# A hybrid decoder layer: the y blocks of the second output half split ahead of the turn, the halo rows turned a tile later

## The chip, the core and the metric

The kernel runs on one core of a Trainium2 chip. The engines that matter here are TensorE (PE in the profile; its weight loads are PEld), VectorE (DVE), ScalarE (ACT) and GpSimd (POOL). All DMAs are issued from the queue of SyncE (SP). The metric is the device time of one execution in microseconds (us); lower is better.

## The reference, cut to what matters

The layer takes 1024 tokens of width 1024, with 16 meta tokens in front (1040 rows in all, float32). It consists of two sub-layers. The first projects the normalised rows and runs two head groups, a state-space mixer (SSD) and a stick-breaking attention (SB); their outputs, each of width 1024, are joined and multiplied by `w_out`, and the normalised product is added to the input. The second is a feed-forward layer with a causal convolution over three rows. The change lies in the end of the first and the way into the second:

```python
y_sb = rms_norm(stick_breaking_attention(q, k, v).reshape(Bsz, L, SB_WIDTH), sb_norm_g[l])
mix = jnp.concatenate([y_ssd, y_sb], axis=-1) @ w_out[l]
h = h + rms_norm(mix, mix_post_g[l])
xn = rms_norm(h, ffn_pre_g[l])
gu = xn @ w_up[l]
g = causal_dwconv(gu[..., :D_FF], ffn_conv_w[l], ffn_conv_b[l])
f = (jax.nn.gelu(g, approximate=True) * gu[..., D_FF:]) @ w_down[l]
```

The convolution looks two rows back, so the first token needs the last two meta rows. These two rows are the "halo" rows below.

## The kernel before, in words

Products of 32-bit accuracy are made of three matmuls: each operand is split into a high part, rounded by a copy on ScalarE, and a low part, the rest, by a subtraction on VectorE or GpSimd; high by high, low by high and high by low are added up in PSUM.

The product with `w_out` is cut into two halves by head group. The first half (SSD) runs among the attention and leaves its result in DRAM (`mixd`). The second half (SB) is the loop around the change, lines 1421 to 1493, over eight tiles t of 128 rows:

- `load_y` (line 929) loads the attention's block of tile t (`yk`, 512 KB) from DRAM. `split_y` makes its high part `yh` on ScalarE (line 938) and its low part `yl` (line 939) on VectorE or GpSimd. The blocks share two SBUF buffers (tag `wraw`) with x tiles 1 and 2 and, later, with weights; `yh` and `yl` have two buffers each.
- `out_steps` (line 951) issues 48 matmuls for a tile, 24 for each half of the columns, in four steps. Its PSUM result `mo` is scaled and added to the mix block `mb` by VectorE (`ev2`, line 1436). PSUM has two banks for `mo`.
- `after` is the norm of a tile in five steps: a square with its sum on ScalarE (line 1120) and a root on GpSimd (lines 191 and 192, `ms_mo` and `rs_mo`); two products on VectorE that give the new h (lines 1123 and 1124) and its store (1126); a second square on ScalarE (1129); a second root on GpSimd (`ms_ff`, `rs_ff`); and the product that gives the normalised rows `oxn` on VectorE (1133).
- `turn_x2`, the "turn", transposes `oxn` on TensorE (line 1139) and takes the result out of PSUM: for tiles 0 to 4 by two pairs of ScalarE copies (1145, 1146), each followed by a subtraction on VectorE (1147). Tile 0 stands for the two halo rows. Both engines read one PSUM tile, and their reads of it follow each other. Tile t is turned in the middle of the matmuls of tile t + 2.

From t = 2 on, TensorE, VectorE, ScalarE and GpSimd run in the order in which the program is written (`manual_schedule`). The order of SP's queue is made by the framework's planner, which issues a load once it reckons that a buffer is free; the queue itself is in order. In iteration t the program writes: the first 24 matmuls of tile t and `ev2`; the second root of norm t - 1; the turn of tile t - 2; the last product of norm t - 1; the split of y block t + 1; steps of the halo rows' own norm (iterations 2 to 4; their sum on VectorE is line 1199); the other 24 matmuls and `ev2`; then the first three steps of norm t. At the end of iteration 4 the halo rows are turned. At iterations 7 and 8 the first weights of the feed-forward are split (lines 1222 and 1223); behind the loop its first products (`g0a`, `u0a`, line 1294) run around the turns of tiles 7 and 8, and the feed-forward's main loop (line 1280) follows.

Of the kernel before, what the change touches and what calls it, by code (L numbers as in the profile page):

```python
# [27 lines left out]
NT = T // P  # L28
# [25 lines left out]
def tile_layer(ctx: ExitStack, tc: tile.TileContext, x, meta, rows, parts,  # L54
               w_z, w_xbc, w_dt, w_q, w_k, w_v, w_out, w_up, w_down, out):
    nc = tc.nc
# [113 lines left out]
    def run(steps, n=None):  # L170
        for _ in steps if n is None else zip(range(n), steps):
            pass
# [705 lines left out]
    def wp_f32(tag, name):  # L878
        return wp.tile([P, 8, P], F32R, tag=tag, name=name, bufs=WB).bitcast(F32).rearrange("p a b -> p (a b)")
# [46 lines left out]
    yraw = [lambda name: wp.tile([P, 8, P], F32, tag="wraw", name=name)]  # L926

    def load_y(half, t, yk):
        nc.sync.dma_start(out=yk, in_=yd1[t - 1] if half else yd[t])
        return yk  # L930

    def split_y(pool, half, t, tags, yk=None, eng=nc.gpsimd):
        nm = f"{half}_{t}"
        if yk is None:
            yk = load_y(half, t, yraw[0](f"yk{nm}"))
        yh = pool.tile([P, 8, P], F32R, tag=tags[0], name=f"yh{nm}", bufs=tags[2])
        yl = pool.tile([P, 8, P], F32R, tag=tags[1], name=f"yl{nm}", bufs=tags[2])
        nc.scalar.activation(yh, yk, AF.Copy)
        eng.tensor_tensor(yl, yk, yh.bitcast(F32), op=ALU.subtract)
        return yh, yl  # L940

    def out_steps(half, t, w, y, evac):
        yh, yl = y
        for hf in range(2):
            acc = psum_mm(f"mo{half}_{t}_{hf}")
            cs = slice(512 * hf, 512 * hf + 512)
            for k, (wh, wl) in enumerate(w):
                if k == 4:
                    yield
                for j, (u, v) in enumerate(((yh, wh), (yl, wh), (yh, wl))):  # L950
                    mm(acc, u[:, k, :], v[:, cs], start=(k == 0 and j == 0), stop=(k == 7 and j == 2))  # L951
            evac(acc, cs)
            yield
# [35 lines left out]
    for p in range(8):  # L989
        for i in range(NT):  # L990
# [30 lines left out]
            if (p, i) == (6, 3):  # L1021
                yk = [load_y(0, 1, rp.tile([P, L + 3], F32, tag="rq", name="yk0_1", bufs=3)[:, :D]
                             .rearrange("p (a b) -> p a b", b=P)),
                      load_y(0, 2, rp.tile([P, L], F32R, tag="rk", name="yk0_2", bufs=3).bitcast(F32)[:, :D]
                             .rearrange("p (a b) -> p a b", b=P))]
# [34 lines left out]
    def psum_fa(name):  # L1060
        return stage[0][1].tile([P, 2, 512], F32, tag="fa", name=name, bufs=3)

    def x2_tiles(t):
        f = psum_fa(f"x2tp{t}")
        return [f[:, hf, :].rearrange("p (b c) -> p b c", c=P) for hf in range(2)]
# [3 lines left out]
    op = opool.enter_context(tc.tile_pool(name="outp", bufs=2, side="right"))  # L1069
# [9 lines left out]
    ys = [split_y(op, 1, 1, ("yh", "yl", 2))]  # L1079
# [114 lines left out]
    def halo_sum(n):  # L1194
        r = (r_ssd, r_ssd, r_sb, r_sb)[n][:2, 0:1]
        if n == 0:
            nc.vector.tensor_scalar(halo_mt, halo_mt, r, None, op0=ALU.mult)
        else:
            nc.vector.scalar_tensor_tensor(halo_mt, halo_mo, r, halo_mt, op0=ALU.mult, op1=ALU.add)
        if n < 3:  # L1200
            nc.sync.dma_start(out=halo_mo, in_=halod[n + 1])
# [10 lines left out]
    def load_raw(j, gu, pool, tag, bufs):  # L1212
        r = pool.tile([P, KB, P], F32, tag=tag, name=f"wr{gu}{j}", bufs=bufs)
        nc.sync.dma_start(out=r, in_=w_up[j, gu])
        raws[gu, j] = r

    def pair_w(nm):
        return [wp.tile([P, KB, P], F32R, tag=f"w{e}", name=f"w{e}{nm}", bufs=WB) for e in ("hi", "lo")]
# [205 lines left out]
    for t in range(1, NT + 1):  # L1424
        if t == 2:
            order.enter_context(tc.manual_schedule(engines=ORDERED))
        if 1 < t < NT - 1:
            yk = load_y(1, t + 1, yraw[0](f"yk1_{t + 1}"))
        if mts:
            mt = mts.pop(0)  # L1430
        else:
            mt = f1.tile([P, 1032], F32, tag="gr", name=f"mb{t}", bufs=2)[:, :D]
            nc.sync.dma_start(out=mt, in_=mixd[t - 1])

        def ev2(acc, cs, mt=mt, t=t):
            nc.vector.scalar_tensor_tensor(mt[:, cs], acc, r_sb[:, t:t + 1], mt[:, cs], op0=ALU.mult, op1=ALU.add)

        if t == 5:
            b22s.append(qp.tile([P, 4, 2 * P], F32, name="b22s", tag="b22s"))
        if t < NT:  # L1440
            xt = wp_f32("wlo", f"xr{t}") if t > 2 else wp.tile([P, D], F32, tag="wraw", name=f"xr{t}")
            nc.sync.dma_start(out=xt, in_=x[(t - 1) * P:t * P, :])
        if t == 7:
            xt8 = qp.tile([P, D], F32, name="xr8", tag="xr8")
            nc.sync.dma_start(out=xt8, in_=x[T - P:, :])
            for jj in range(2):
                load_raw(jj, 0, wp, "wraw", 2)
        steps = out_steps(1, t, wres2, ys.pop(0), ev2)
        run(steps, 2)
        run(norm, 1)  # L1450
        if len(pend) > 1:
            turn = pend.pop(0)()
            run(turn, 2)
            run(norm)
            if t == NT:
                run(steps)
            run(turn)
        run(norm)
        if 1 < t < NT - 1:
            ys.append(split_y(op, 1, t + 1, ("yh", "yl", 2), yk, nc.vector if t < 5 else nc.gpsimd))  # L1460
        if t == 2:
            halo_sum(2)
        elif t == 3:
            halo_sum(3)
            halo_norm = after(0, halo_mt, 2, halo_xt, halo_mo, halo_mo)
            run(halo_norm, 1)
        elif t == 4:
            run(halo_norm)
        if t == 7:
            g0.split_1()  # L1470
            load_raw(0, 1, wp, "wraw", 2)
        elif t == NT:
            g0_pair = pair_w("2g0")
            u0.split_1()
            g0.split_2(g0_pair)
            load_raw(1, 1, wp, "wraw", 2)
        run(steps)
        if t == 6:
            edge_x2()
        if t == NT:  # L1480
            break
        if t == 6:
            ys.append(split_y(op, 1, NT, ("yh", "yl", 2)))
        xn = f1.tile([P, 1032], F32, tag="fa", name=f"oxn{t}")[:, :D]
        junk = psum_fa(f"jk{t}").rearrange("p a b -> p (a b)")
        norm = after(t, mt, P, xt, xn, junk)
        run(norm, 1)
        if t == 7:
            xt = xt8
        run(norm, 2)  # L1490
        pend.append(lambda t=t, xn=xn: turn_x2(t, P, xn, x2_tiles(t)))
        if t == 3:
            run(halo_norm, 2)
        elif t == 4:
            run(turn_x2(0, 2, halo_mo, x2_tiles(0)))
    opool.close()
    tA, tB = ExitStack(), ExitStack()
# [372 lines left out]
```

## Time and profile before

| | us |
|---|---|
| median of 3 runs | 1745.74 |
| the runs | 1743.22, 1745.74, 1745.97 |
| the profiled execution | 1741.94 |
| its span | 1740.0 |
| TensorE busy in it | 1707.8 |
| TensorE's longest wait in the second output half | 5.94 |

A row of the order of time gives start and length in us, the engine, the line of the kernel, what is written from what, and in brackets the idle time ahead of it with what ended it. Tile numbers are left out of names. A row of waits gives who waited for whom, the total in us, how often, and the longest. A row of a stretch gives the stretch, its length, the busy time of TensorE, its weight loads, VectorE, ScalarE and GpSimd with their instruction counts, the clock granted to TensorE (1.00 is full), the busy share of the DMA engines and their GB/s. "SPq" is SP issuing a DMA.

### The profile page before, as it was taken

How to read it: one execution, taken by the hardware profiler on the slowest of the kernel's cores; microseconds unless marked ns; L12 is line 12 of the kernel's file. 1: busy time of each engine (PE TensorE's matmuls, PEld its weight loads, DVE VectorE, ACT ScalarE, POOL GpSimd, SP SyncE). 2: the span in 40 equal slices, each digit the busy share in tenths (PEclk: the TensorE clock that was granted, in tenths of full speed). 3: DMA queues.
4: the chain of work that ended last, by engine and by line, in shares of the span. 5: the costliest groups of instructions: out<-in, count | busy, mean ns of one | idle time of the engine just before them, and what ended most of it. 6: DMA issues, size and time to landing. Idle time of an engine off the chain costs nothing.

```text
span 1740.0 us, 28052 instructions
## 1 busy us (share of the span) xinstructions
PE 1707.8 (98%) x11230; PEld 1496.6 (86%) x11230; DVE 1121.2 (64%) x1230; ACT 822.9 (47%) x1374; POOL 857.9 (49%) x645
## 2 busy tenths in 40 slices
PE   7999999999999999999999979999999999999998
PEld 6999889888999998998687768999988888887886
DVE  5752964775676677668532457676666666658777
ACT  5423653545566566558553234533333333343544
POOL 4323663686565566555552124487776777400001
PEclk9999999999999999999999999999999999999999
DMA  4233343231011011122215443232332222395335
GB/s 163 63 110 98 98 135 109 65 95 38 26 37 45 30 37 32 31 62 73 82 57 199 165 145 122 67 116 97 105 108 91 92 91 91 108 322 199 104 110 181
DMA packets 90694, 173.88 MB, mean 100 GB/s; under 512 B 10714, under 2 KB 35834, under 8 KB 90564
## 3 DMA queue, kind: packets, MB, share of 16 engines
q1 hardware_dynamic: 90564, 172.10, 31.2%
q8 instruction: 88, 1.44, 0.4%
q14 instruction: 42, 0.34, 0.1%
HBM read 122.33 MB, written 49.73 MB: 99 GB/s over the span
## 4 chain that ended last, share of the span: by engine, by line
PE 89%; issue 3%; DVE 3%; ACT 2%; POOL 2%; DMA 1%; POOLq 0%; DVEq 0%; SPq 0%; ACTq 0%
PE fX L1280 10%; PE dnA L1690 7%; PE fY L1280 6%; PE fA L1280 6%; PE mo L951 6%; PE pj_k L165 5%; PE pj_v L165 5%; PE pj_z L165 5%; PE dnB L1690 5%; PE pj_q L165 5%; PE pj_X L165 5%; PE av L802 4%; PE z L765 3%; PE tw L787 3%; PE pj_B L165 1%
## 5 line engine op out<-in xcount | busy, mean ns | idle before, releaser
L775 POOL TENSOR_TENSOR bt<-bt,kp 128x256 f32<-128x256 f32 (+7 forms) x128 | 213.0, 1683 | 185.5 <-DVE kp L773 135.2
L773 DVE TENSOR_TENSOR_SCAN kp<-kp,hold 128x272 f32<-128x272 f32 (+7 forms) x128 | 183.4, 1473 | 25.3 <-ACT kp L766 15.0
L1223 POOL TENSOR_TENSOR wlo<-wr,whi 128x1024 fp32r<-128x1024 f32 x43 | 107.9, 2518 | 38.4 <-ACT whi L1222 38.4
L1727 POOL TENSOR_TENSOR fms<-fms 128x1 f32<-128x1 f32 x8 | 3.2, 394 | 223.4 <-ACT dh L1612 197.0
L766 ACT ACTIVATE kp<-z 128x288 f32<-128x288 f32 (+6 forms) x112 | 82.6, 737 | 50.9 <-PE z L765 27.5
L1222 ACT ACTIVATE whi<-wr 128x1024 fp32r<-128x1024 f32 x43 | 45.6, 1060 | 111.6 <-PE fX L1280 68.3
L165 PE MATMUL pj_v<-xs,wh_v 128*128 128x400 f32 (+2 forms) x384 | 94.9, 334 | 0.0
L1352 DVE SCALAR_TENSOR_TENSOR ga<-gr,pp,ga 128x1024 f32<-128x1024 f32 x44 | 72.3, 1643 | 34.9 <-ACT ga L1345 34.1
L165 PE MATMUL pj_k<-xs,wh_k 128*128 128x400 f32 (+2 forms) x384 | 94.5, 333 | 0.0
L165 PE MATMUL pj_q<-xs,wh_q 128*128 128x386 f32 (+2 forms) x384 | 93.9, 331 | 0.0
L789 ACT ACTIVATE th<-tw 128x1024 f32<-128x1024 f32 (+2 forms) x96 | 75.6, 816 | 38.5 <-PE tw L787 38.4
L1612 ACT ACTIVATE dh<-ar 128x512 fp32r<-128x512 f32 x77 | 48.5, 630 | 92.7 <-PE dnB L1690 44.7
L165 PE MATMUL pj_X<-xs,wh_X 128*128 128x400 f32 (+2 forms) x384 | 92.0, 327 | 0.2 <-ACT craw_X L211 0.2
L165 PE MATMUL pj_z<-xs,wh_z 128*128 128x386 f32 (+2 forms) x384 | 91.5, 326 | 0.0
L951 PE MATMUL mo<-woa,yh 128*128 128x512 f32 x256 | 84.4, 398 | 2.1 <-ACT ma L963 1.2
L1613 DVE TENSOR_TENSOR dl<-ar,dh 128x512 fp32r<-128x512 f32 x77 | 53.2, 692 | 50.4 <-ACT dh L1612 50.3
L741 DVE CAST qh<-q 128x128 fp32r<-128x128 f32 x64 | 45.7, 715 | 59.7 <-PE z L765 59.4
L767 ACT ACTIVATE bt<-z 128x288 f32<-128x288 f32 (+6 forms) x112 | 82.9, 740 | 0.0
L802 PE MATMUL av<-th,v 128*64 128x128 f32 x1152 | 77.2, 278 | 0.0
L787 PE MATMUL tw<-ident,bt 128*128 128x128 f32 x576 | 75.7, 274 | 0.9 <-ACT bt L767 0.5
L802 PEld LDWEIGHTS av<-th,v 128*64 128x64 f32 x1152 | 61.5, 136 | 13.8 <-issue 11.1
L787 PEld LDWEIGHTS tw<-ident,bt 128*128 128x128 f32 x576 | 65.5, 141 | 7.1 <-issue 3.3
(558 smaller groups left out, 5648.8 us busy)
## 6 DMA issues: line engine op xcount, KB each, us to landing
wr<-in_w_up SPq DMA_DIRECT2D x44, 512.0 KB
fds<-ga SPq DMA_DIRECT2D x44, 256.0 KB
b<-in_w_down SPq DMA_DIRECT2D x44, 256.0 KB
ar<-fds SPq DMA_DIRECT2D x44, 256.0 KB
fda<-ga SPq DMA_DIRECT2D x33, 256.0 KB
ar<-fda SPq DMA_DIRECT2D x33, 256.0 KB
yk<-yd SPq DMA_DIRECT2D x16, 512.0 KB
wor<-in_w_out SPq DMA_DIRECT2D x12, 512.0 KB
```

Source lines behind the costliest of these rows:

```text
L165: mm(acc[:ncol, :n - s], a[:, k, :ncol], xs[c0][:, b, k, s:n], start=(k == 0 and j == 0), stop=(k == KB - 1 and j == 2))
L766: nc.scalar.activation(kp[:, :, a:a + w], z[:, :, :w], AF.Sigmoid, scale=-QSCALE)
L767: nc.scalar.activation(bt[:, :, a:a + w], z[:, :, :w], AF.Sigmoid, scale=QSCALE)
L773: nc.vector.tensor_tensor_scan(kp[:, j][:, ::-1], kp[:, j][:, ::-1], hold[:, L - n:L][:, ::-1], 0.0, op0=ALU.mult, op1=ALU.max)
L775: nc.gpsimd.tensor_tensor(bt[:, j, 0:m], bt[:, j, 0:m], kp[:, j, 1:m + 1], op=ALU.mult)
L787: nc.tensor.transpose(tw[:, j, b, :], bt[:, j, c0:c0 + P], ident)
L789: nc.scalar.activation(th[:, :, :nb, :], tw[:, :, :nb, :], AF.Copy)
L802: mm(av[halves[j], :], v[:, kb, halves[j]], th[:, j, b, :], start=kb == 0, stop=kb == i)
L951: mm(acc, u[:, k, :], v[:, cs], start=(k == 0 and j == 0), stop=(k == 7 and j == 2))
L1223: nc.gpsimd.tensor_tensor(l, raw, h.bitcast(F32), op=ALU.subtract)
L1280: mm(acc[:, c, :nn], u[:, k, :], v[:, k, c0:c0 + nn], start=first and k == 0 and j == 0, stop=k == 3 and j == 2, skip_group_check=not first)
L1690: mm(banks[BANK[n], t], u[:, 0, c], v[:, 1, :], start=(n in (1, 2, 5) and p == 0 and i == 0), stop=(p == NPR - 1 and i == 2), skip_group_c ...
```

## The change

Three pieces of the loop are written at other places. The load of block 3 is written in iteration 1, ahead of the tile's other loads, and the load of block t + 2 in iteration t, behind the split of block t + 1 (before: block t + 1 at the head of iteration t). The split of block t + 1 is written ahead of the turn of tile t - 2 and of the last product of norm t - 1. The turn of the halo rows is written at the end of iteration 5. The last split, of block 8, stays where it was and takes the block that is already loaded.

```diff
     for t in range(1, NT + 1):
         if t == 2:
             order.enter_context(tc.manual_schedule(engines=ORDERED))
-        if 1 < t < NT - 1:
-            yk = load_y(1, t + 1, yraw[0](f"yk1_{t + 1}"))
+        if t == 1:
+            yk = load_y(1, 3, yraw[0]("yk1_3"))
...
         steps = out_steps(1, t, wres2, ys.pop(0), ev2)
         run(steps, 2)
         run(norm, 1)
+        if 1 < t < NT - 1:
+            ys.append(split_y(op, 1, t + 1, ("yh", "yl", 2), yk, nc.vector if t < 5 else nc.gpsimd))
+            yk = load_y(1, t + 2, yraw[0](f"yk1_{t + 2}"))
         if len(pend) > 1:
             turn = pend.pop(0)()
             run(turn, 2)
...
             run(turn)
         run(norm)
-        if 1 < t < NT - 1:
-            ys.append(split_y(op, 1, t + 1, ("yh", "yl", 2), yk, nc.vector if t < 5 else nc.gpsimd))
         if t == 2:
             halo_sum(2)
...
         if t == 6:
-            ys.append(split_y(op, 1, NT, ("yh", "yl", 2)))
+            ys.append(split_y(op, 1, NT, ("yh", "yl", 2), yk))
...
         if t == 3:
             run(halo_norm, 2)
-        elif t == 4:
+        elif t == 5:
             run(turn_x2(0, 2, halo_mo, x2_tiles(0)))
```

## The prediction

> **What bounds the kernel now.** I read the page first, then TensorE's own waits over the second output half (955 to 1130 us), then the order of time on each engine there.
>
> ```profile
> span 1740.0 us, 28052 instructions
> ...
> PE 1707.8 (98%) x11230; PEld 1496.6 (86%) x11230; DVE 1121.2 (64%) x1230; ACT 822.9 (47%) x1374; POOL 857.9 (49%) x645
> ```
>
> TensorE is the bound of the whole, so a change can only win where TensorE stands still. In this stage it does so for a named cause (engine, line, releaser: total, times, longest):
>
> ```profile
> PE x2tp L1139 <- DVE mo L1133: 5.9, 1, 5.9
> ...
> PE fX L1280 <- POOL wlo L1223: 0.2, 1, 0.2
> ```
>
> The first is the turn of the halo rows behind tile 4. The second is all that TensorE waits for between this stage and 1130. In order of time (start, length, in brackets the wait ahead) come three more, for the low part of a y block:
>
> ```profile
> 1003.76 0.50 PE L951 MATMUL mo<-wohb,yl 128*128 128x512 f32 x1 [1.49 <-DVE yl L939]
> ...
> 1015.23 0.39 PE L951 MATMUL mo<-wolb,yh 128*128 128x512 f32 x1
> ...
> 1021.56 0.98 PE L1139 MATMUL x2tp<-ident,mo 2*128 2x2 f32 x8 [5.94 <-DVE mo L1133]
> ...
> 1029.76 0.49 PE L1139 MATMUL x2tp<-ident,oxn 128*128 128x128 f32 x3
> ...
> 1037.96 0.50 PE L951 MATMUL mo<-wohb,yl 128*128 128x512 f32 x1 [1.46 <-POOL yl L939]
> ...
> 1043.33 1.03 PE L1139 MATMUL x2tp<-ident,oxn 128*128 128x128 f32 x8
> ...
> 1049.67 0.39 PE L951 MATMUL mo<-wohb,yh 128*128 128x512 f32 x1
> ...
> 1051.54 0.50 PE L951 MATMUL mo<-wohb,yl 128*128 128x512 f32 x1 [1.48 <-POOL yl L939]
> ...
> 1075.02 0.28 PE L1294 MATMUL g0a<-b11h,whi 128*128 128x258 f32 x1
> ...
> 1087.42 1.03 PE L1139 MATMUL x2tp<-ident,oxn 128*128 128x128 f32 x8
> ```
>
> 1003.76, 1037.96 and 1051.54 are the second matmul of tiles 4, 6 and 7 (the first needs only the high part). 1029.76, 1043.33 and 1087.42 are the turns of tiles 3, 4 and 8, 1075.02 is the first matmul behind the loop. From a tile's second matmul to its turn goes 5.37 (1037.96 to 1043.33), from there to the next tile's first matmul 6.34 (to 1049.67).
>
> The long wait also costs clock. TensorE's granted clock is the 1.00 and the 0.78 behind the five engines' busy times:
>
> ```profile
> 995.00:1005.00 10.00, 8.51 (x42) 6.82 (x41) 7.06 (x9) 4.30 (x8) 0.79 (x2) 1.00 0.43 137
> ...
> 1019.00:1019.50 0.50, 0.00 (x0) 0.00 (x0) 0.50 (x2) 0.00 (x0) 0.00 (x0) 0.78 0.00 0
> ```
>
> It falls some 3.6 after the last matmul ended (1015.23 + 0.39 = 1015.62). From the halo transposes to turn 3 then go 8.20 (1021.56 to 1029.76), where 0.6 for the transposes, 0.3 and 5.37 make 6.3: 1.9 lost to it. The 1.49 wait inside 995 to 1005 leaves it at 1.00.
>
> **The change part by part.** Nothing is added or removed in amount: the same loads, splits and transposes. Three things move.
>
> (a) The y loads are written earlier. Their queue is not ordered by hand, and what gates them is a buffer: y4's load went out at 989.88 and y6's at 1003.74, each when the split before it (yl) let go of one of two buffers.
>
> ```profile
> 989.88 0.32 SPq L929 DMA_DIRECT2D yk<-yd  x1
> ...
> 1002.49 1.22 DVE L939 TENSOR_TENSOR yl<-yk,yh 128x1024 fp32r<-128x1024 f32 x1
> ...
> 1003.74 0.32 SPq L929 DMA_DIRECT2D yk<-yd  x1
> ...
> 1000.54 1.06 ACT L938 ACTIVATE yh<-yk 128x1024 fp32r<-128x1024 f32 x1
> ```
>
> The split of y6's predecessor starts 1002.49, lasts 1.22, the load follows at once. So the loads move only as far as the splits do. I cost them at nothing: y4's load is 10.66 ahead of its first use at 1000.54. If that cover were gone, ScalarE would stand with the turn queued behind the split; the third rival prices such a case. y3's load moves ahead of tile 1's x load in the same way, and y8's split only finds its block loaded.
>
> (b) The split (ScalarE L938, then the low part on VectorE for y3 to y5, on GpSimd for y6 and y7) goes from behind the turn's copies and the norm to directly behind the previous tile's second square (ScalarE L1129). (c) The halo transposes go behind tile 5 and their copies behind tile 5's second square. On VectorE yl moves past the turn's two low parts and the norm's last product, which from now on stand behind it while it waits for yh; behind them stands the evacuation of the tile's second half. On GpSimd it moves past nothing: one norm's step is ahead of it and the next one's behind it, as before. Rows that carry the walk:
>
> ```profile
> 996.55 1.03 ACT L1129 ACTIVATE jk<-mb 128x1024 f32<-128x1024 f32 x1 [3.65 <-DVE mb L1124]
> ...
> 1004.97 1.06 ACT L1120 ACTIVATE mo<-mb 2x1024 f32<-2x1024 f32 x1 [3.37 <-issue]
> ...
> 1006.03 1.00 ACT L1120 ACTIVATE jk<-mb 128x1024 f32<-128x1024 f32 x1
> ...
> 1013.23 1.06 ACT L1129 ACTIVATE mo<-mb 2x1024 f32<-2x1024 f32 x1 [1.26 <-POOL ms_ff L191]
> ...
> 1017.07 1.06 ACT L938 ACTIVATE yh<-yk 128x1024 fp32r<-128x1024 f32 x1
> ...
> 1026.98 1.03 ACT L1129 ACTIVATE jk<-mb 128x1024 f32<-128x1024 f32 x1 [3.66 <-DVE mb L1124]
> ...
> 1033.65 1.06 ACT L938 ACTIVATE yh<-yk 128x1024 fp32r<-128x1024 f32 x1
> ...
> 1034.79 3.12 POOL L939 TENSOR_TENSOR yl<-yk,yh 128x1024 fp32r<-128x1024 f32 x1 [5.70 <-ACT yh L938]
> ...
> 1042.04 1.03 ACT L1129 ACTIVATE jk<-mb 128x1024 f32<-128x1024 f32 x1 [3.65 <-DVE mb L1124]
> ...
> 1003.62 1.27 DVE L1199 SCALAR_TENSOR_TENSOR mb<-mo,r_sb,mb 2x1024 f32<-2x1024 f32 x1
> ```
>
> Steps read from rows: ScalarE's next instruction starts 1.06 behind a square (1004.97 to 1006.03); yl starts 1.14 behind yh (1033.65 to 1034.79); TensorE starts 1.27 behind a yl on VectorE (1002.49 to 1003.76), 3.17 behind one on GpSimd (1034.79 to 1037.96).
>
> Tile 4: yh at 996.55 + 1.06 = 997.6, yl 998.8, TensorE 1000.0. It asks at 1003.76 - 1.49 = 1002.3, so the 1.49 goes, with 2.3 to spare. The price: the turn's copies start about 1.0 later, but 1.14 of yl no longer stands ahead of the halo sum (1003.62); I take 0.5 earlier for all that follows on the halo's chain (between 0 and 1.14).
>
> Tile 5: TensorE no longer meets the halo turn. It comes to the second matmul at 1015.62 - 1.49 + 0.2 = 1014.3 (the second follows the first by less than a matmul's 0.39). The y5 split now stands behind the halo's second square: 1013.23 - 0.5 + 1.06 = 1013.8, yl 1014.9, TensorE 1016.2. A new wait of 1.9 takes the place of 5.94 and of the slow clock. Turn 3 then starts at 1016.2 + 5.37 = 1021.6 against 1029.76: 8.2 gained.
>
> Tile 6: 1021.6 + 6.34 = 1027.9, then the halo transposes. They took 0.98 at the low clock; between half of that and all of it, I take 0.6. TensorE asks for the low part at 1028.8. Norm 4's second square is 0.5 earlier, 1026.5; yh 1027.6; yl on GpSimd 1028.7; TensorE 1031.9. New wait 3.1; gain 1037.96 - 1031.9 = 6.1. Here VectorE and ScalarE, not TensorE, set the time.
>
> Tile 7: TensorE at 1031.9 + 5.37 + 6.34 + 0.3 = 1043.9. Turn 3's four copies, which began about 1.1 behind the transposes of 1029.76, now begin behind yh at 1028.6: 2.2 earlier; and VectorE no longer waits 0.6 for TensorE's second half (as the row at 1049.87 below shows for tile 6). So tile 5's norm comes some 2.9 earlier, ScalarE's 1042.04 becomes 1039.1; the halo's small copies now follow that square (0.5, between 0 and 0.7), yh 1040.7, yl 1041.8, TensorE 1045.0. Wait 1.1, gain 6.5. The loop's end follows as before, 23.48 later: 1068.5 against 1075.02.
>
> Behind the loop TensorE needs tile 8's norm for its turn, 12.40 behind the loop's end: at 1080.9. That norm is on a chain through VectorE, ScalarE and GpSimd:
>
> ```profile
> 1049.87 0.75 DVE L1436 SCALAR_TENSOR_TENSOR mb<-mo,r_sb,mb 128x512 f32<-128x512 f32 x1 [0.62 <-PE mo L951]
> ...
> 1054.86 1.28 DVE L1123 SCALAR_TENSOR_TENSOR mb<-mb,rs_mo,gpost 128x1024 f32<-128x1024 f32 x1 [0.57 <-POOL rs_mo L192]
> ...
> 1076.43 2.39 POOL L1223 TENSOR_TENSOR wlo2g<-wr,whi2g 128x1024 fp32r<-128x1024 f32 x1
> ...
> 1079.88 0.22 POOL L191 TENSOR_SCALAR ms_mo<-oss 128x1 f32<-128x1 f32 x1 [1.05 <-ACT t4l L1120]
> ...
> 1085.59 1.28 DVE L1133 SCALAR_TENSOR_TENSOR oxn<-mb,rs_ff,gffn 128x1024 f32<-128x1024 f32 x1 [0.45 <-POOL rs_ff L192]
> ...
> 1099.75 1.06 ACT L1222 ACTIVATE whi<-wr 128x1024 fp32r<-128x1024 f32 x1 [2.33 <-PE g0c L1294]
> ```
>
> From norm 6 on (1054.86) this chain waits for itself more than for TensorE. Turn 4's copies started about 1.1 behind the transposes of 1043.33 and now start behind yh7, at 1041.7: 2.7 earlier. Two waits of 0.6 go too: 1049.87's for TensorE, which is now ahead, and 1054.86's for GpSimd, which y8's split held up. I take 4.0 from norm 6 on. The second of the two weight splits before norm 8 then ends at 1078.8 - 4.0 = 1074.8, and norm 8's first GpSimd step starts right there, 5.1 before 1079.88. So oxn starts at 1080.5 in place of 1085.59, and its transposes at 1081.9 (the 1.28 of its row and 0.1): a fourth new wait, 1.0. Gain 1087.42 - 1081.9 = 5.5. After that the next weight split waits for TensorE itself (1099.75, L1294), so VectorE's and GpSimd's later work moves along with it and the gain stays.
>
> Sum: removed 1.49 + 5.94 + 1.46 + 1.48 and 1.9 of slow clock, 12.3. Added 1.9 + 3.1 + 1.1 + 1.0 = 7.1. By waits 5.2, by positions 5.5 (a wait is counted from a matmul's modelled end, which lies behind the next one's start); I take the positions. The profiled run took 1741.94, its span of 1740.0 and 1.94 around it; it becomes 1736.4. It lies 3.8 under the median of the three runs; from that median, 1745.74 - 5.5 = 1740.2. No change is anything within 0.2%, 3.5 us, about what runs from 1743.22 to 1745.97 can tell.
>
> The clock against a rule. The new wait at tile 6 is 3.1 with one matmul in it, shorter than the 3.6 after which the row shows the fall. The Trainium skill, "TensorE: Matmul & The Clock Gate", Part 1 (What's actually happening), says an idle window of about 3.4 us halves the clock, and that windows run freely. The trace agrees in its one fall here. If it counted this wait as idle, tile 6 would lose up to the 1.9 of the row above. By that rule TensorE comes to tile 7 at 1045.8 in place of 1043.9, 0.8 behind the low part that it waits for, and the sum is between 4.7 and 5.5 (the wait at tile 8's turn can take the 0.8 up); by the row it is 5.5.
>
> **The rivals.**
>
> TensorE alone sets the pace: the other engines, freed of queueing, catch up at tiles 6, 7 and 8, and only tile 5's 1.9 remains. 12.3 - 1.9 = 10.4, 1735.3. For it: VectorE is busy only 64%. Against it: norm 4's second square (1026.98) lies 11.4 behind the end of tile 4's matmuls, so the norms already trail TensorE by a tile.
>
> The gain is given back at the turn of tile 8. If norm 6 moves only by its two waits, 1.2 to 2 in place of 4.0, oxn gains 3.1 at most and so does the end: 1742.6, no measurable change. For it: tile 8's norm already ends only 0.55 before TensorE asks (1085.59 + 1.28 against 1087.42).
>
> Slower: a y load at the head of SP's queue holds the loads behind it.
>
> ```profile
> SPq L929 <- POOL yl L939: 10.2, 1, 10.2
> ...
> 1037.93 0.32 SPq L929 DMA_DIRECT2D yk<-yd  x1
> ...
> 1038.35 0.38 SPq L1433 DMA_DIRECT2D mb<-mixd  x1
> ...
> 1042.00:1042.50 0.50, 0.50 (x4) 0.42 (x3) 0.00 (x0) 0.46 (x1) 0.00 (x0) 1.00 0.11 41
> ```
>
> Here y8's load stood 10.2 for a buffer and tile 6's mix block (mixd) went out right behind it; both had landed by 1042, where the DMA share falls to 0.11. If the new order puts a load there whose buffer only yl7 frees (1041.8 + 3.1 = 1044.9), the mix block lands some 4 later, at 1049, instead of before VectorE comes to it, behind norm 5's additions and the halo's small low parts at about 1040.8, and tile 6's chain is 8.2 late: 8.2 - 5.5 = 2.7 slower, 1748.4. It decides once that block is issued after 1036.8. Against it: two buffers, one held by y7, leave y8 only the one that yl6 frees at 1031.9.
>
> The change doesn't do what it says for the loads, by (a); that alters no time and is in the forecast.
>
> **How the numbers follow.** Forecast 0.74, 1740.2; its own range, with 1.5 for the halo chain, the halo turn and GpSimd's 2.4 to 3.1 per split, and 1 for the median: 1738.2 to 1742.2. TensorE alone 0.05; given back at tile 8 0.14; slower 0.07. Faster is the first two, 0.79; same 0.14; slower 0.07. The range 1737.8 to 1743.6 leaves out TensorE alone, slower and part of the third.
>
> **What would show it.** Right: no wait of TensorE for the halo's oxn (DVE mo L1133); waits for yl at tiles 5, 6 and 7 of about 2, 3 and 1; a new wait for oxn at tile 8 of about 1; clock 1.00 through 1015 to 1026; y4's and y6's loads only some 3 earlier. Wrong: a wait for mb or yk loads on VectorE or ScalarE, a clock below 1 behind tile 6, or the halo's second square not earlier than now.

## The result, and the profile after

The changed kernel takes 1737.4 us, median of 5 runs (1735.0 to 1738.5), against 1745.74 of before (5 runs beside it, 1743.2 to 1747.3): ratio 0.9952, 95% interval 0.9938 to 0.9967. It is faster, as forecast, but by 8.3 in place of 5.5: 1737.4 lies 0.4 below the low end of the range. Half a per cent is small, but the interval stays clear of 1. Two more sets gave 1736.7 (9 runs, ratio 0.9961, 0.9948 to 0.9973) and 1738.8 (5 runs, 0.9963, 0.9950 to 0.9976).

The page of the profiled run (1737.67; before 1741.94):

```profile
span 1735.8 us, 28056 instructions
...
PE 1709.0 (98%) x11230; PEld 1497.3 (86%) x11230; DVE 1115.8 (64%) x1230; ACT 822.7 (47%) x1374; POOL 858.2 (49%) x645
```

The instruction counts of the five engines are those of before, and so are the busy times within 1.3, but for VectorE's, which is 5.4 less: some of its instructions became shorter, 2.2 of it a single one (L1173, below). The rest of what changed is waits. TensorE's own waits, 955 to 1130, after (total, times, longest):

```profile
PE mo L951 <- POOL yl L939: 1.4, 2, 0.9
PE x2tp L1139 <- DVE oxn L1133: 1.0, 1, 1.0
PE mo L951 <- ACT yh L938: 0.8, 1, 0.8
PE mo L951 <- DVE yl L939: 0.8, 1, 0.8
...
PE fX L1280 <- POOL wlo L1223: 0.2, 1, 0.2
```

The 5.9 for the halo's mo is gone. In its place stand small waits: tile 5 waits for yh and yl, tiles 6 and 7 for GpSimd's yl, the turn of tile 8 for oxn. In order of time (TensorE, after):

```profile
1017.04 0.51 PE L951 MATMUL mo<-wohb,yh 128*128 128x512 f32 x1 [0.82 <-ACT yh L938]
1018.30 0.50 PE L951 MATMUL mo<-wohb,yl 128*128 128x512 f32 x1 [0.75 <-DVE yl L939]
...
1025.25 1.04 PE L1139 MATMUL x2tp<-ident,oxn 128*128 128x128 f32 x8
...
1031.68 0.65 PE L1139 MATMUL x2tp<-ident,mo 2*128 2x2 f32 x8
...
1033.24 0.50 PE L951 MATMUL mo<-wohb,yl 128*128 128x512 f32 x1 [0.48 <-POOL yl L939]
...
1046.25 0.50 PE L951 MATMUL mo<-wohb,yl 128*128 128x512 f32 x1 [0.94 <-POOL yl L939]
...
1069.77 0.28 PE L1294 MATMUL g0a<-b11h,whi 128*128 128x258 f32 x1
...
1083.38 1.06 PE L1139 MATMUL x2tp<-ident,oxn 128*128 128x128 f32 x8 [1.04 <-DVE oxn L1133]
```

The two profiles don't reach the stage at the same time. VectorE's token sum (L448), which stands ahead of everything the change touches, in the profile of before:

```profile
968.42 0.14 DVE L448 TENSOR_SCALAR tmsb<-ptb 2x1 f32<-2x1 f32 x1 [8.93 <-PE ptb L445]
```

and after:

```profile
970.81 0.15 DVE L448 TENSOR_SCALAR tmsb<-ptb 2x1 f32<-2x1 f32 x1 [8.98 <-PE ptb L445]
```

So 2.39 is taken off a time of after when it is compared with one of before or of the prediction. What I call the walk is the distance from this row to the turn of tile 8: 1087.42 - 968.42 = 119.00 before, 1083.38 - 970.81 = 112.57 after, 6.4 less. The spans differ by 4.2 only, since this run came 2.4 later to the stage.

### The profile page after: what moved, and what is told of

Same layout as the page of the kernel before. It is cut to its first block, busy times and chain, and to the rows that moved or that the text cites. A ratio compares the mean times of both kernels' runs of the same rounds, so it can differ in the third digit from the quotient of the medians.

```text
span 1735.8 us, 28056 instructions
## 1 busy us (share of the span) xinstructions
PE 1709.0 (98%) x11230; PEld 1497.3 (86%) x11230; DVE 1115.8 (64%) x1230; ACT 822.7 (47%) x1374; POOL 858.2 (49%) x645
```

## The experiments

Distances from the start of the stage (L448), one profiled run each. The columns are the turn of tile 8 and the first matmul of `g0c`, the feed-forward product that follows it. From there to the end of the span, 645.6 to 646.1 pass in every profiled run but fill_wait's (650.7), so what a kernel gains here it keeps.

| kernel | turn of tile 8 | first g0c matmul | ratio to before, 95% interval |
|---|---|---|---|
| before, two profiles | 119.00, 119.63 | 125.52, 126.15 | |
| loads_only | 119.16 | 125.67 | 1.0001, 0.9992 to 1.0010 |
| halo_later | 117.05 | 123.56 | 0.9989, 0.9980 to 0.9997 |
| split_ahead | 115.67 | 122.20 | 0.9981, 0.9971 to 0.9990 |
| fill_wait | 118.51 | 125.02 | 1.0012, 1.0001 to 1.0022 |
| fill_matmul | 116.87 | 123.38 | 0.9988, 0.9979 to 0.9996 |
| after, three profiles | 112.57, 112.55, 112.50 | 119.11, 119.14, 119.10 | 0.9952, 0.9961, 0.9963 |
| square_later | 112.31 | 118.85 | 0.9951, 0.9939 to 0.9963 |
| vector_low | 112.85 | 119.39 | 0.9949, 0.9936 to 0.9962 |
| norm8_first | 112.47 | 119.02 | 0.9959, 0.9946 to 0.9971 |
| both | 112.03 | 118.63 | 0.9951, 0.9939 to 0.9964 |
| both_norm8 | 110.96 | 120.78 | 0.9965, 0.9953 to 0.9977 |
| both_norm8_early | 110.91 | 117.45 | 0.9951, 0.9937 to 0.9964 |

**The parts of the change, one at a time.** The y loads alone, on before:

```diff
-        if 1 < t < NT - 1:
-            yk = load_y(1, t + 1, yraw[0](f"yk1_{t + 1}"))
+        if t == 1:
+            yk = load_y(1, 3, yraw[0]("yk1_3"))
...
             ys.append(split_y(op, 1, t + 1, ("yh", "yl", 2), yk, nc.vector if t < 5 else nc.gpsimd))
+            yk = load_y(1, t + 2, yraw[0](f"yk1_{t + 2}"))
...
         if t == 6:
-            ys.append(split_y(op, 1, NT, ("yh", "yl", 2)))
+            ys.append(split_y(op, 1, NT, ("yh", "yl", 2), yk))
```

> The changed places of the y loads alone (y3 ahead of tile 1's x block, each later one right behind a split), with the splits behind the turn's copies and the halo rows turned behind tile 4 as before. Theory: the loads go out when a buffer comes free, not when they are written, so the time is that of before within 0.5, and the four waits stay 1.49, 5.94, 1.46 and 1.48 within 0.3. Rival: the loads were late in the runs that the profile does not show; gain 1 or more.

119.16 against 119.00, the waits again 1.5, 6.0 and 1.5 twice. Costing the loads at nothing was right.

The splits alone, on before (the two lines of the split moved from behind `run(norm)` to behind `run(norm, 1)`):

```diff
         run(norm, 1)
+        if 1 < t < NT - 1:
+            ys.append(split_y(op, 1, t + 1, ("yh", "yl", 2), yk, nc.vector if t < 5 else nc.gpsimd))
         if len(pend) > 1:
...
         run(norm)
-        if 1 < t < NT - 1:
-            ys.append(split_y(op, 1, t + 1, ("yh", "yl", 2), yk, nc.vector if t < 5 else nc.gpsimd))
```

> Before, with the splits ahead of the turn, the loads written where they were and the halo rows turned behind tile 4 as before. Theory: TensorE comes to the halo's turn 1.5 earlier, but the halo's norm is only 0.5 earlier, so the wait there grows from 5.94 to about 6.9 and the clock falls as before; the waits of 1.46 and 1.48 at tiles 6 and 7 go or shrink below 0.7. Gain 0.5 + 1.46 + 1.48 = 3.4 at most, and no less than 2: about 1742.5. Rival: the low parts only wait because TensorE is early after the halo's turn, and another wait takes their place; gain under 1.

TensorE in that run:

```profile
1020.28 0.98 PE L1139 MATMUL x2tp<-ident,mo 2*128 2x2 f32 x8 [6.97 <-DVE mo L1133]
...
1083.57 1.07 PE L1139 MATMUL x2tp<-ident,oxn 128*128 128x128 f32 x8 [0.29 <-DVE oxn L1133]
```

The wait for the halo grew to 6.97 (6.9 expected), all waits for low parts are gone, and the walk is 3.3 shorter (3.4 at most expected). Tile 4's 1.49 was worth little while the halo's turn stood behind it: turn 3 starts 61.1 from the start of the stage, 61.3 before.

The halo's turn alone, on before:

```diff
-        elif t == 4:
+        elif t == 5:
             run(turn_x2(0, 2, halo_mo, x2_tiles(0)))
```

> Before, with the halo rows turned one tile later and nothing else. Theory (the walk): the wait of 5.94 goes, but y5's split still stands behind turn 2's copies and the norm (ScalarE 1017.07), so TensorE waits at tile 5's second matmul until 1017.07 + 1.14 + 1.27 = 1019.5, 3.7 long, and turn 3 starts between 1024.9 and 1026.8, 3.0 to 4.9 before 1029.76. At tiles 4, 6 and 7 the waits for low parts stay at 1 to 1.5, because their splits follow the turns. Gain at the end 3 to 4.5, about 1742. Rival: the halo's wait was the whole matter; then the gain is that of the full change, 6 to 8.

```profile
1021.02 0.80 PE L951 MATMUL mo<-wohb,yh 128*128 128x512 f32 x1 [2.56 <-ACT yh L938]
...
1023.13 0.79 PE L951 MATMUL mo<-wohb,yl 128*128 128x512 f32 x1 [1.31 <-DVE yl L939]
...
1030.64 1.03 PE L1139 MATMUL x2tp<-ident,oxn 128*128 128x128 f32 x8
```

The walk is 2.0 shorter, less than the 3 to 4.5 expected. The waits at tile 5 add up to 3.9 (3.7 expected) and behind them TensorE's clock is about half until 1028: from the second matmul to turn 3 go 7.5 where 5.37 do at full clock. I had left the fall open (up to 1026.8 for turn 3; 1027.8 in the times of before was measured). Of the 5.94 that the move takes away, two thirds come back as waits for a split that still stands late. The two parts alone give 2.0 + 3.3 = 5.3 of the 6.4; together they save one more: split_ahead leaves the halo's wait and halo_later the waits for late splits, and after has little of either.

**The clock behind the halo's turn.** Two runs fill the old wait with work for TensorE, on before. First with transposes:

```diff
         elif t == 4:
-            run(turn_x2(0, 2, halo_mo, x2_tiles(0)))
+            tps0 = x2_tiles(0)
+            for i in range(40):
+                nc.tensor.transpose(tps0[i // 4 % 2][:, i % 4, :], ident, ident)
+            run(turn_x2(0, 2, halo_mo, tps0))
```

> Before, with 40 transposes of the unit matrix ahead of the halo's turn, into the same PSUM tile, which the real ones overwrite: about 0.13 each, 5.2 in all, so that TensorE is busy through most of its 5.94 wait. Its output is unchanged. Theory: the halo's transposes start where they did, TensorE's clock stays at 1.00 behind them, so turn 3 comes 1.5 to 2.1 earlier and, since y6's split follows turn 3, tiles 6 and 7 and the turn of tile 8 too: gain 1.5 to 2, about 1742.7. Rival: the clock's share is not on the path, the waits at tiles 6 and 7 take it up; gain under 0.5.

TensorE, and a window behind it (the granted clock is the 0.69 behind the five engines' busy times):

```profile
1022.94 0.65 PE L1139 MATMUL x2tp<-ident,mo 2*128 2x2 f32 x8 [1.46 <-DVE mo L1133]
...
1030.70 1.04 PE L1139 MATMUL x2tp<-ident,oxn 128*128 128x128 f32 x8
```

```profile
1024.00:1026.00 2.00, 2.00 (x8) 1.61 (x7) 0.21 (x1) 0.80 (x2) 0.80 (x2) 0.69 0.44 178
```

This miss is instructive. The transposes were shorter than I took them for (4.5, not 5.2), 1.46 of waiting was left, and behind it and the 0.65 of tiny halo transposes the clock fell all the same. The walk gained 0.5 only. That the profiled run was slower in all has another place: a wait of 3.6 for VectorE's gr (L1331) at 1144, which no other profile has. VectorE itself stood there 3.1 for a store to land (`fda`, ahead of L1404; 0.9 in before), though the store went out as in before. Why it landed late stays open.

Then with matmuls that leave no gap:

```diff
+        if t == 4:
+            y4 = ys[0][0]
...
         elif t == 4:
-            run(turn_x2(0, 2, halo_mo, x2_tiles(0)))
+            f0 = psum_fa("x2tp0")
+            for i in range(26):
+                mm(f0[:, 0, :], y4[:, 0, :], wres2[0][0][:, :512], start=True, stop=True)
+            run(turn_x2(0, 2, halo_mo, [f0[:, hf, :].rearrange("p (b c) -> p b c", c=P) for hf in range(2)]))
```

> Before, with 26 matmuls of 128x512 (0.227 each, 5.9 in all) ahead of the halo's turn, into the same PSUM tile, which the transposes overwrite; its output is unchanged. The 40 transposes left 1.46 of the wait and the clock fell behind that. Theory: with no idle time left the clock stays at 1.00 through 1030, the halo's transposes start within 0.5 of where they did, turn 3 comes 1.5 to 2.0 earlier against the start of the stage, and the waits of 1.46 and 1.48 stay, so the turn of tile 8 comes 1.2 to 2.0 earlier: that is the clock's share of the loss at the halo's turn. Rival: the waits at tiles 6 and 7 grow by as much, and turn 8 gains under 0.5.

```profile
1018.69 6.05 PE L1499 MATMUL x2tp<-wohb,yh 128*128 128x512 f32 x26
1024.72 0.65 PE L1139 MATMUL x2tp<-ident,mo 2*128 2x2 f32 x8
...
1030.88 1.04 PE L1139 MATMUL x2tp<-ident,oxn 128*128 128x128 f32 x8
```

From the halo's transposes to turn 3 go 6.2 (8.2 before), the clock stays at 1.00, and the turn of tile 8 comes 2.1 earlier, with the waits of 1.5 at tiles 6 and 7 unchanged. The ratio, 0.9988, agrees. So the clock's share of the old loss is 2.1 (1.9 in the prediction), and it can be had by burning the wait with useless matmuls.

**What bounds the changed kernel.** The halo's second square behind the split, on after:

```diff
         if t == 3:
-            run(halo_norm, 2)
+            run(halo_norm, 1)
```

> The changed kernel, with the second square of the halo's norm moved from the end of tile 3's step behind turn 2's copies in tile 4's step, so that y5's split no longer stands behind it. Theory: y5's high part comes 1.06 earlier, TensorE's two waits at tile 5 (0.82 for yh, 0.75 for yl) shrink to 0.5 at most together, its clock stays at 1.00 there, and turn 3 comes 2 to 2.7 earlier against the start of the stage. But tile 6's low part hangs on ScalarE's and VectorE's chain (norm 4's second square, 1028.64), which is not earlier, so the wait there grows from 0.48 to 2.5 to 3.2, and the turn of tile 8 is where it was within 0.5: no gain. Rival: the clock lost at tile 5 reaches the end; then turn 8 comes 1.6 to 2.7 earlier and the time is about 1735.

```profile
1023.31 1.03 PE L1139 MATMUL x2tp<-ident,oxn 128*128 128x128 f32 x8
...
1033.72 0.80 PE L951 MATMUL mo<-wohb,yl 128*128 128x512 f32 x1 [1.93 <-POOL yl L939]
...
1041.71 1.04 PE L1139 MATMUL x2tp<-ident,oxn 128*128 128x128 f32 x8
```

Tile 5's waits are gone but for 0.17 and turn 3 is 3.3 earlier (51.2 from the start of the stage, 54.4 after). At tile 6 TensorE waits 0.31, 0.29 and 1.93, now it is there that the clock falls (from turn 3's 1023.31 to turn 4's 1041.71 go 18.4, in after 13.4), and at the turn of tile 8 0.3 is left of the 3.3. TensorE now waits at tile 6 for the low part, which the other engines set, as the prediction had it.

The changed kernel's third profile shows the same without any edit:

> The changed kernel a third time, beside the next run and with another set of runs of before. Theory: of the 2.8 to 3.5 by which its median lay under the forecast, 0.9 is the walk (6.4 in place of 5.5) and 1.2 the three runs' median of before, which lies that much above the median of 32 (1744.5); the rest is how many half-clock stretches fell into the few runs compared. So the median here lies between 1736.5 and 1738.5 and turn 8 at 112.5 from the start of the stage again. Rival: some gain behind the turn of tile 8 is missed; then the median is 1737 or less again and the distance from the turn of tile 8 to the end of the span is shorter than before's by 0.7 or more with as many stretches.

```profile
1018.32 0.50 PE L951 MATMUL mo<-wohb,yl 128*128 128x512 f32 x1 [0.76 <-DVE yl L939]
...
1023.67 1.03 PE L1139 MATMUL x2tp<-ident,oxn 128*128 128x128 f32 x8
...
1033.24 0.50 PE L951 MATMUL mo<-wohb,yl 128*128 128x512 f32 x1 [1.93 <-POOL yl L939]
```

The waits at tile 5 are those of the first profile (0.80 and 0.76), but here the clock stayed at 1.00: turn 3 is 5.35 behind the second matmul, in the first profile 6.95. The 1.6 went straight into tile 6's wait (1.93 for 0.48), and turn 8 is at 112.50, as in the other two. The distance from g0c to the end, 645.6, is no shorter than before's 646.1 by anything like the rival's 0.7: no gain is hidden behind the turn of tile 8. The median came out 0.3 above the 1736.5 to 1738.5 expected.

The second profile, with the same waits and the same fall of the clock as the first:

> The changed kernel once more, for what varies from run to run. Its first profile gained 6.4 at the turn of tile 8 against the profile of before once both are laid on the start of the stage (VectorE's first token sum, 968.42 and 970.81), and lost 2.4 ahead of the change. Theory: the 6.4 belongs to the change and comes again, 6 to 7; the 2.4 ahead of it is a run's own, so here it lies anywhere from 0 to 3, and the ratio is about 0.995. Rival: the 2.4 belongs to the new program (its instructions lie at other places); then it comes again within 0.3.

6.4 came again. The 2.4 ahead of the stage came too (971.49), which alone would speak for the rival; but halo_later and before's second profile, programs that are the same as before up to there, reached the stage at 971.26 and 970.36, and vector_low, which begins like after, at 968.67. It is a run's own.

The low parts of y6 and y7 on VectorE, on after:

```diff
-            ys.append(split_y(op, 1, t + 1, ("yh", "yl", 2), yk, nc.vector if t < 5 else nc.gpsimd))
+            ys.append(split_y(op, 1, t + 1, ("yh", "yl", 2), yk, nc.vector))
```

> The changed kernel, with the low parts of y6 and y7 on VectorE (1.27 each) in place of GpSimd (2.4 each). Theory: the waits of 0.48 and 0.94 at tiles 6 and 7 go to 0.3 at most and the loop ends about 1.1 earlier, but VectorE, on whose chain norm 8 hangs, carries 2.5 more, so the wait at the turn of tile 8 grows from 1.04 to between 2.1 and 4.5, and the time is between that of the changed kernel and 2.4 more. Rival: what GpSimd is late with is what sets the end; then turn 8 comes 1.0 to 1.4 earlier.

```profile
1081.52 1.06 PE L1139 MATMUL x2tp<-ident,oxn 128*128 128x128 f32 x8 [1.52 <-DVE oxn L1133]
```

The loop ends 1.1 earlier, tile 7's wait is 0.63, and turn 8 is 0.3 later: the wait there grew by 0.5 (2.1 to 4.5 were expected in all, 1.52 came), and 0.45 for `wlo2g`, the low part of a feed-forward weight block, came ahead of it. What TensorE gains at tiles 6 and 7 doesn't reach the turn of tile 8.

Norm 8 ahead of half a weight split on GpSimd, on after:

```diff
-            g0.split_2(g0_pair)
+            w2 = raws[0, 1]
+            nc.scalar.activation(g0_pair[0], w2, AF.Copy)
+            lo2 = [(g0_pair[1][:, k], w2[:, k], g0_pair[0][:, k].bitcast(F32)) for k in (LO4, HI4)]
+            nc.gpsimd.tensor_tensor(*lo2[0], op=ALU.subtract)
+            g0.w["a21"], g0.w["a22"] = [(g0_pair[0][:, k], g0_pair[1][:, k]) for k in (LO4, HI4)]
...
-    run(norm, 2)
+    run(norm, 1)
+    nc.gpsimd.tensor_tensor(*lo2[1], op=ALU.subtract)
+    run(norm, 1)
```

> The changed kernel, with the second half of the low part of the weight block split on GpSimd ahead of norm 8 (wlo2g, 2.87) moved behind norm 8's first GpSimd step, so that this step starts when ScalarE's square is done (1074.5) and not at 1076.23. Theory: oxn of tile 8 comes 1.5 earlier, the wait of 1.04 at the turn of tile 8 goes, and that turn and all behind it come 1.0 earlier: about 1736. Rival: another wait stands right behind (the half moved is late for its matmuls, or VectorE is), and nothing is gained.

VectorE and GpSimd in that run:

```profile
1078.84 2.30 DVE L1123 SCALAR_TENSOR_TENSOR mb<-mb,rs_mo,gpost 128x1024 f32<-128x1024 f32 x1 [2.15 <-ACT b22h L1156]
```

```profile
1078.77 1.29 POOL L1533 TENSOR_TENSOR wlo2g<-wr,whi2g 128x512 fp32r<-128x512 f32 x1
```

The rival held. Norm 8's product started 1.1 earlier against the stage, but with the moved half beside it on GpSimd it took 2.30 in place of 1.28. Nothing was left.

Both edits that shorten the loop (the halo's square, the low parts on VectorE) together:

> The changed kernel with the halo's second square later and with the low parts of y6 and y7 on VectorE. Theory: no wait at tile 5, its clock at 1.00; at tile 6 the low part comes 1.1 earlier than in the run with the later square alone, so 0.8 is left of 1.93 and the clock does not fall there either; the loop ends 2 to 3.5 earlier than in the changed kernel, but norm 8 still waits for GpSimd's two weight splits behind the loop, and the turn of tile 8 comes 0 to 1.5 earlier only, with a wait of 2 to 4: 1735 to 1737. Rival: VectorE's chain is late by its 2.5 more, and turn 8 is as late as in the run with low parts on VectorE alone or later (112.8 from the start of the stage).

No fall of the clock, waits of 0.76, 0.75 and 1.49 at tiles 6, 7 and at the turn of tile 8, the loop 1.9 shorter (97.1 against 99.0; 2 to 3.5 expected), turn 8 0.5 earlier. The chain to norm 8, not TensorE, takes the rest. Then, with `split_2` taken apart as in norm8_first, the second half on VectorE:

```diff
     split_x("t1", 0, 258, nc.vector)
     run(turn7, 1)
+    nc.vector.tensor_tensor(*lo2[1], op=ALU.subtract)
```

> The run above, and the second half of wlo2g's low part taken from GpSimd to VectorE behind the first low part of t1, where no GpSimd work runs beside norm 8's product (which took 2.30 in place of 1.28 with the half moved on GpSimd). Theory: GpSimd reaches norm 8 1.1 to 1.5 earlier, the product keeps its 1.28, so the turn of tile 8 comes 1.0 to 1.5 earlier than in the run above, 1 to 3 earlier than in the changed kernel: 1734 to 1736. Rival: as with the half moved on GpSimd, something else takes it up, and turn 8 stays within 0.3.

```profile
1082.05 0.58 PE L1294 MATMUL g0a<-b21h,wlo2g 128*128 128x258 f32 x1 [1.55 <-DVE wlo2g L1544]
```

The turn came 1.1 earlier, but I had the use of that half in the wrong place: it is wanted right behind the turn, TensorE waited 1.55 behind the turn's own 1.14, the clock fell, and g0c is 2.2 later than in the run above. Put behind oxn instead:

```diff
     run(norm)
+    nc.vector.tensor_tensor(*lo2[1], op=ALU.subtract)
     split_x("t1", 0, 258, nc.vector)
     run(turn7, 1)
-    nc.vector.tensor_tensor(*lo2[1], op=ALU.subtract)
```

> The last run with the moved half of wlo2g's low part on VectorE right behind oxn of tile 8 and ahead of t1's low part, since its matmuls, which I had taken for later ones, stand right behind the turn of tile 8 and waited 1.55 for it. Theory: it is ready 0.7 before they ask, the wait of 1.55 and the half clock from 1080 to 1086 go, the turn of tile 8 stays at 111.0 and the first matmul of g0c comes 1.0 to 1.5 earlier than in the changed kernel: about 1735.5. Rival: t1's low part, 0.7 later, is waited for instead, and g0c comes no earlier.

Turn 8 at 110.91, g0c at 117.45, no wait for wlo2g: 1.7 less than after in the walk. Its time, 1736.7 (5 runs, ratio 0.9951), can't be told from after's.

Before once more:

> Before once more, for its run-to-run spread (1741.2 to 1747.9). Theory: it comes from stretches of about 4 in which the clock is half without a long wait ahead, at places that differ from run to run (54, 416, 810, 880 in the runs so far). Taken without the walk (span less the distance from the start of the stage to the turn of tile 8), the runs stand at 1620.1 and 1621.0 with no such stretch, and 1 to 2.5 higher for each. So this run's rest is 1621 plus 1 to 2.5 for each stretch that its clock shows outside the walk, and inside the walk it repeats the first profile within 0.3: waits 1.49, 5.94, 1.46, 1.48 and half clock from 1018 to 1026. Rival: the rest is that of the first profile, whatever its clock shows.

1742.5 - 119.6 = 1622.9 beside 1621.0 of the first profile, and one half-clock stretch (from 879 to 883) more, as expected. Inside the walk the waits repeat, but against the start of the stage the half clock came and went 1.3 later, so less of it fell into the wait: turn 8 is 0.6 later, outside the 0.3 expected. As a rule for every run the price per stretch is too simple: both_norm8 has a stretch at 55 and reached the stage at 968.2 all the same.

## Why the prediction was right, and where it was wrong

**Bound and mechanism: right.** The halo's wait went (halo_later) and the share of the clock behind it, 2.1 (fill_matmul), though tile 5 took 1.6 of clock back. The waits for low parts shrank, and the four places where new waits were forecast are the four that have them: 1.6 at tile 5 (1.9 forecast), 0.48 at tile 6 (3.1), 0.94 at tile 7 (1.1), 1.04 at the turn of tile 8 (1.0). Tile 6's is short because the slow clock at tile 5 held TensorE back by 1.6 and the low part came 1.05 early; without the fall it is 1.93 (after's third profile).

**Loads: right.** They moved only with the splits: y4's went out at 989.41 - 2.39 = 987.0 (989.88 before), and nothing depends on it.

**Tile 5: right in place, wrong on the clock.** The second matmul is at 1015.9 (1016.2 forecast). That the clock stays at 1.00 behind it was wrong in four of five profiles with these waits and right in one. It costs 1.6 there and nothing at the end, because tile 6 waits longer anyway; that it did no harm to the sum was luck.

**Tile 6: a term taken too long.** The walk put the low part's 3.17 on GpSimd behind yl's start and came to 1031.9; TensorE was there at 1030.85. The row of before was y6's, and VectorE's product of the norm stood beside it:

```profile
1034.40 1.28 DVE L1133 SCALAR_TENSOR_TENSOR oxn<-mb,rs_ff,gffn 128x1024 f32<-128x1024 f32 x1
```

GpSimd, in the changed kernel:

```profile
1030.82 2.37 POOL L939 TENSOR_TENSOR yl<-yk,yh 128x1024 fp32r<-128x1024 f32 x1
...
1043.81 2.39 POOL L939 TENSOR_TENSOR yl<-yk,yh 128x1024 fp32r<-128x1024 f32 x1 [0.68 <-ACT yh L938]
...
1047.57 3.16 POOL L939 TENSOR_TENSOR yl<-yk,yh 128x1024 fp32r<-128x1024 f32 x1 [1.38 <-ACT yh L938]
```

The subtraction takes 2.4 here and took 3.12 in the row of before; y8's, which now runs beside a norm's product (oxn, from 1047.19), takes 3.16. It is the same in all sixteen profiles: 3.12 to 3.16 where this product starts 0.4 ahead of the subtraction, 2.36 to 2.41 where it doesn't run beside it. Moving the split ahead of the norm's last product took away not only the queueing but the neighbour that slowed it. I took the duration from a row whose surroundings the change removes. The prediction had 2.4 as the other end of its range and chose the wrong one; 0.75 there, and 0.3 on yl's start, make the 1.05 by which tile 6 was early. Tile 7 (1043.9 for 1045.0) and the loop's end (1067.4 for 1068.5) carry it on. The turn of tile 8 doesn't, because it waits for its norm and not for TensorE.

**From norm 6 on: the step that failed.** The 5.5 of the sum is the turn of tile 8, and that hung on "I take 4.0 from norm 6 on", made of turn 4's copies (2.7) and two waits of 0.6. It was 5.5: VectorE's product of norm 6 moved from 1054.86 to 1051.72 - 2.39 = 1049.33. Its root stands on GpSimd behind y8's low part, and what that split costs was read from VectorE's wait of 0.57 alone. The rows of before:

```profile
1049.92 1.06 ACT L938 ACTIVATE yh<-yk 128x1024 fp32r<-128x1024 f32 x1 [1.64 <-issue]
...
1051.51 2.37 DVE L1173 TENSOR_TENSOR xa<-xa 128x8 f32<-128x8 f32 x1
...
1053.94 0.23 POOL L191 TENSOR_SCALAR ms_mo<-oss 128x1 f32<-128x1 f32 x1
```

and of after:

```profile
1046.44 1.06 ACT L938 ACTIVATE yh<-yk 128x1024 fp32r<-128x1024 f32 x1
...
1051.72 1.28 DVE L1123 SCALAR_TENSOR_TENSOR mb<-mb,rs_mo,gpost 128x1024 f32<-128x1024 f32 x1 [0.39 <-POOL rs_mo L192]
...
1073.28 2.87 POOL L1223 TENSOR_TENSOR wlo2g<-wr,whi2g 128x1024 fp32r<-128x1024 f32 x1
...
1076.23 0.22 POOL L191 TENSOR_SCALAR ms_mo<-oss 128x1 f32<-128x1 f32 x1
```

Before, y8's high part stood 1.64 and started 0.1 behind the end of tile 6's last matmul, which I take for the wait for one of the two yh buffers. TensorE has left tile 6 earlier now, the high part follows turn 4's copies at once, and y8's low part ends at 1050.73 - 2.39 = 1048.3 instead of 1053.9, 5.5 earlier. VectorE's row showed only 0.57 of it because VectorE was late there itself: its tiny L1173 took 2.37 beside that low part (0.15 now). Against it, wlo2g took 2.87 in place of 2.39, so norm 8's first step on GpSimd is 6.0 earlier and not 5.1: that is the 0.9 by which the walk gained 6.4 in place of 5.5 (turn of tile 8 at 1081.0 for 1081.9).

From the end of y8's low part to the turn of tile 8 go 32.6 in after's three profiles and in split_ahead, square_later, vector_low and both alike (32.61 to 32.65), 33.6 before. So y8's split, and not the low parts of y6 and y7, sets the end of these kernels: vector_low makes those earlier and the turn of tile 8 later.

**The wait at tile 8's turn: right in size by luck.** 1.04 measured, 1.0 forecast, but both its ends were forecast 0.9 too late, TensorE's by tile 6's low part and oxn's by norm 6. What holds it is GpSimd's queue ahead of norm 8, as both_norm8_early shows: without half of wlo2g the turn is 1.1 earlier than in the run with both edits.

**The clock rule: neither price was paid.** By the row the sum was 5.5, by the rule of the Trainium skill ("TensorE: Matmul & The Clock Gate", Part 1, What's actually happening: free-running windows, an idle one halves the clock) 4.7 to 5.5 through a fall at tile 6. The traces agree with free-running windows (last section) and not with the idle one: the fall came at tile 5, behind a window of 3.41 in which TensorE was busy for 1.84, and it did not reach the end.

**The base: the other term that failed.** The sum was hung on 1745.74. In the four later sets before's median was 1744.4 to 1744.6 (32, 17, 19 and 9 runs), 1.2 lower: the median of three runs was too few to hang 5.5 on. With 1744.5 and the walk's 6.4 comes 1738.1. The three medians of after are 1736.7, 1737.4 and 1738.8, median of all 19 runs 1737.5; what is left is 0.6. Part of it can be the walk of before, which its first profile shows at its shortest (119.00, against 119.16 and 119.63 in loads_only and the second profile). How much the number of half-clock stretches in these few runs adds stays open.

**The rivals.** TensorE alone as the pace (1735.3) and the gain given back at tile 8 (1742.6) did not come, nor a load that stands in the way: VectorE and ScalarE never waited for an mb or yk load.

## What to carry to other kernels

A duration from a row holds for the row's neighbours: where engines slow each other, ask what runs beside it after the move, not before. A wait in a row is only what was left over once everything else had been late: norm 6's 0.57 stood for a split that came 5.5 earlier, so walk the split itself. When a wait is taken away, walk on to the next in-order chain and price what it can give; here splits and halo turn were worth 3.3 and 2.0 alone, and shortening TensorE's path in the loop further gave 0.5 at most, because y8's split and the chain behind it to norm 8 set the time. Hang a small forecast on as many runs as there are: three runs were 1.2 off, more than the 0.9 by which the walk was.

## What the hardware did that I had not expected

Short waits can halve TensorE's clock, and so, it seems, can tiny matmuls. The half clock comes in windows: in all sixteen profiles every half-clock stretch but the last, which runs past the kernel's end, lasts 3.41, 6.83 or 10.24, and the starts within one run lie whole multiples of 3.413 apart (after: 879.09 and 1019.04, 41 windows). Where the windows lie against the kernel differs from run to run. Around tile 5 in after (the granted clock is the 1.00 and the 0.50 behind the five engines' busy times):

```profile
1015.63:1019.04 3.41, 1.84 (x7) 1.01 (x6) 1.83 (x2) 2.47 (x6) 0.77 (x2) 1.00 0.19 76
1019.04:1022.45 3.41, 3.41 (x9) 2.66 (x9) 2.45 (x3) 0.93 (x2) 0.00 (x0) 0.50 0.49 154
```

Counted so over the walk in all sixteen profiles, TensorE is busy for 1.85 or less in the window ahead of a fall and for 1.86 or more in the windows that none follows. The two exceptions, falls behind 1.95 (fill_wait) and 2.02 (square_later), hold the halo's 2x2 transposes. So a wait counts by how much of it one window catches: in the third profile of after tile 5's window begins 0.4 to 0.7 earlier against the stage than in the four runs that fell, and has 1.86. How sharp this limit is was not tried.

The half-clock stretches outside the walk stand where TensorE looks fully busy, right behind a group of matmuls with one to sixteen columns, or (at 810 to 816) behind short waits. In the third profile of after, TensorE and then three stretches behind (the granted clock is the 0.95, the 0.50 and the 0.69 behind the five engines' busy times):

```profile
52.41 2.09 PE L543 MATMUL tpd<-fold,dtT 32*16 32x16 f32 x18
```

```profile
54.00:56.00 2.00, 2.00 (x13) 1.97 (x13) 2.00 (x3) 1.98 (x3) 0.99 (x1) 0.95 0.83 252
56.00:58.00 2.00, 2.00 (x8) 1.99 (x7) 2.00 (x1) 0.50 (x1) 1.38 (x1) 0.50 0.05 18
58.00:60.00 2.00, 2.00 (x10) 1.99 (x9) 2.00 (x3) 0.00 (x0) 0.00 (x0) 0.69 0.79 205
```

Further on in the same run:

```profile
415.27 2.07 PE L445 MATMUL pta<-ones,sq 128*2 128x1 f32 x18
```

```profile
418.00:420.00 2.00, 2.00 (x14) 1.43 (x11) 0.60 (x3) 1.80 (x4) 1.50 (x1) 0.50 0.00 0
```

and in the second profile of before:

```profile
876.25 1.94 PE L860 MATMUL avm<-wcm,meta_v 16*128 16x4 f32 x16
```

```profile
880.00:882.00 2.00, 2.00 (x17) 1.67 (x18) 0.19 (x1) 2.00 (x4) 0.47 (x3) 0.50 0.65 172
```

The first profile of before has the same three groups, and 1.00 in the same windows. So some 2 of idle or thin work is enough in some runs and not in others: the waits of 1.49 at tiles 4, 6 and 7 never did it, 1.46 with 0.65 of 2x2 transposes behind did (fill_wait), 0.8 and 0.75 with a matmul between did four times in five. A stretch of 3.41 at half clock costs up to 1.7 where TensorE is the bound (1.6 at tile 5). That thin matmuls are the cause was not tried by itself; it is where the falls stand.
